# The output stage's tile transposes: from TensorE to VectorE's 32x32 blocks, with the rest of the turn done by the store to DRAM

## The chip, the core and the metric

The kernel runs on one core of a Trainium2 chip. The core has five engines with queues of their own: TensorE (PE, matrix products; PEld is its weight load), VectorE (DVE), ScalarE (ACT), GpSimd (POOL) and SyncE (SP, which here issues DMAs only), and 16 DMA engines that all queues share. The metric is device time in microseconds. The time before is 2435.05 us, the median of three runs (2434.82 to 2436.79).

## The reference, cut to what matters

One layer of a hybrid streaming encoder, for 2048 prompt rows and 8 x 16 sample rows that share the parameters: 17 tiles of 128 rows, 1024 features. A gated DeltaNet group and a short convolution make a 1024-wide row per token. Then, in float32:

```python
mix = jnp.concatenate([o, sc_out.astype(x.dtype)], axis=-1) @ w_o
x = x + rmsnorm(mix, norm_mix_post)

h = rmsnorm(x, norm_ffn_pre)
f = (jax.nn.silu(h @ w_gate) * (h @ w_up)) @ w_down
x = x + rmsnorm(f, norm_ffn_post)
```

The change lies between the second and the last but one of these lines: h, scaled by norm_ffn_pre, has to stand with features on the partitions (transposed) for the products with w_gate and w_up.

## The kernel before

The kernel goes through three parts: projection and recurrence (to about 860 us), the output stage (17 tiles, lines 1116 to 1433), and the feed-forward part (gate and up products in three groups of row tiles, lines 1297 to 1545, then the down products).

**The output stage.** `o_load(t)` (1155) has SP load the mixed rows of tile t into `mr` (one buffer, two halves) and the rows of x into `xo` (two buffers). `o_tile(t)` (1169) casts and splits `mr` into high and low parts (`mix_split`, 1127: ScalarE casts `mh`, VectorE subtracts to `ml`; three buffers each), loads for t+1, and runs 48 products of 128x128 with 128x512 into two PSUM banks, one of `psd` (three banks) and one of `tbank` (two). Then ScalarE sums the squares (1185), VectorE and GpSimd form the factor (`rstd`, 151), and VectorE scales (1190) and adds into `xo` (1191), which ScalarE's queue stores as `x2d` (1192). `o_rows` (1198) makes h of it: squares (1200), factor, `hx = xo * r` (1204). Then come eight TensorE transposes of 128x128 into two PSUM banks (1210), two evictions by VectorE which multiply by the norm weights `g_ffn` on the way (1211) into `ht` (one buffer), and one store from ScalarE's queue into the DRAM tile `hTd` (1214), in runs of 128 floats.

**hTd and its readers.** The 17 tiles form three groups of 6, 6 and 5 (`FGROUPS`); each has one `hTd` with features on the partitions. `ffn_load` (1297) reads it back, eight loads per group, each of 128 features by all rows of the group. The feed-forward products use seven matrix combinations instead of eight (names B11, T3, T1, T2, B21, T4, B22): `ffn_sums` and `ffn_prep` (1308, 1320) form sums and differences of blocks of h and split each into high and low parts.

**The order.** The first group is loaded after tile 6 and is prepared in seven steps, one after each of tiles 7 to 13 (1350 to 1355), each step ordered behind the last tile's work on ScalarE and VectorE by `issue_after`. Groups 1 and 2 are loaded inside the loop over f of the group before (f = 4 to 11), and their sums are formed at f = 12, 14, 16 and 18. The last tile's `o_rows` runs after the first step of the feed-forward loop (1507). In each step f (`gate_up`, 1437) ScalarE copies three partial products out of PSUM (1448 to 1450) before TensorE adds four more products each into those banks (1454 to 1456); two SiLUs follow (1462, 1467), the second marked `gmark["A"]`. Each engine runs its own instructions in order; the order between them is made by a scheduler from the program's order and these marks.

Of the kernel before, what the change touches and what calls it, by code (L numbers as in the profile page):

```python
# [9 lines left out]
F32 = mybir.dt.float32  # L10
F32R = mybir.dt.float32r
BF16 = mybir.dt.bfloat16
AF = mybir.ActivationFunctionType
# [4 lines left out]
P = 128  # L18
D = 1024
KD = D // P  # L20
# [49 lines left out]
FGROUPS = [list(range(0, 6)), list(range(6, 12)), list(range(12, 17))]  # L70
# [27 lines left out]
def kernel(  # L98
# [24 lines left out]
    nc = tc.nc  # L123
    V, A, G, T = nc.vector, nc.scalar, nc.gpsimd, nc.tensor

    const = ctx.enter_context(tc.tile_pool(name="const", bufs=1))
    dram = ctx.enter_context(tc.tile_pool(name="dram", bufs=1, space=DRAM))
# [1 line left out]
    mixo = [dram.tile([P, H, P], F32, name=f"mixo{t}") for t in range(NT)]  # L129
    mixs = [dram.tile([P, 4, len(g) * P], F32, name=f"mixs{gi}") for gi, g in enumerate(GROUPS)]  # L130
    wsplit = [dram.tile([P, 2, KD, P], F32, name=f"wsplit{j}") for j in range(28)]
    hTd = [dram.tile([P, KD, len(g) * P], F32, name=f"hTd{gi}") for gi, g in enumerate(FGROUPS)]
    partd = [[dram.tile([len(g) // 2, P, 7, len(c) // 2, P], F32, name=f"partd{gi}_{ch}") for ch, c in enumerate(FCHUNKS)]
             for gi, g in enumerate(FGROUPS)]
    lastd = [dram.tile([P, 2, len(c) // 2, P], F32, name=f"lastd{ch}") for ch, c in enumerate(FCHUNKS)]
# [5 lines left out]
    ident, ones = cst[:, 0:128], cst[:, 128:256]  # L141
# [3 lines left out]
    g_ffn = vec[:, 8:16]  # L145
# [5 lines left out]
    def rstd(small, ss, n, scale, eps, tag):  # L151
        m = small.tile([P, n], F32, tag=tag[0] + "m", name=tag + "m")
        V.tensor_scalar(out=m, in0=ss, scalar1=scale, scalar2=eps, op0=ALU.mult, op1=ALU.add)
        r = small.tile([P, n], F32, tag=tag + "r", name=tag + "r")
        G.tensor_tensor(out=r, in0=m, in1=neghalf[:, :n], op=ALU.pow)
        return r
# [9 lines left out]
    with ExitStack() as ph:  # L166
# [690 lines left out]
        def new_group(gi, hi, lo, rb):  # L857
            tiles = GROUPS[gi]
            g = dict(gi=gi, tiles=tiles, n=len(tiles), npr=sum(t != SAMPLE for t in tiles), hi=hi, lo=lo, rb=rb,
                     kT=[], qT=[], dt=[], ssk=sm("ssk"), ssq=sm("ssq"),  # L860
                     kt=gp.tile([P, H, MAXT, P], F32, tag="kt", name="kt"),
                     vt=gp.tile([P, H, MAXT, P], F32, tag="vt", name="vt"),
                     sz=gp.tile([P, H, W1], F32, tag="sz", name="sz"))
            return g
# [93 lines left out]
        n = len(tiles)  # L958
        c = n * P
# [31 lines left out]
        for w2 in w2s:  # L991
            j = order.pop(0)[0]
# [74 lines left out]
        for gi, tiles in enumerate(GROUPS):  # L1067
            if gi == 1:
                events.setdefault(30, []).append(caches)
            g = new_group(gi, hi, lo, rb)  # L1070
# [6 lines left out]
            c = len(tiles) * P  # L1077
            for slot, j in enumerate(SEQS[min(gi, 2)]):
# [3 lines left out]
                ps = firsts[slot] if early else psd.tile([P, 512], F32, tag="d", name="dbank")  # L1082
                for s, ks in enumerate((range(0, 3), range(3, 6), range(6, 8))):
                    if not early:
                        matmuls(ps, w, hi, lo, c, ks)
                    if s == 2:
                        later = finish_block(j, ps, g)
                        if later:
                            kind, h = BLOCKS[j]
# [16 lines left out]
        for t in sorted(events):  # L1106
            for f in events[t]:
# [8 lines left out]
        op = ps_o.enter_context(tc.tile_pool(name="op", bufs=1, reuse_waits="tile", side="right"))  # L1116
        oa = ps_a.enter_context(tc.tile_pool(name="oa", bufs=1, reuse_waits="tile", side="right"))
        pft = ps_p.enter_context(tc.tile_pool(name="pft", bufs=3, space=PSUM, reuse_waits="tile"))
        gpost = op.tile([P, D], F32, name="gpost")
        ojunk = op.tile([P, 512], BF16, name="ojunk")  # L1120
        spare = [op.tile([P, D], F32, tag="hx", name="hx"), op.tile([P, KD, P], F32, tag="ht", name="ht"),
                 oa.tile([P, KD, P], F32, tag="mr", name="mr")]
        wo = {k: [oa.tile([P, D], F32R, name=f"{nm}{k}") for nm in ("woh", "wol")] for k in reversed(range(KD))}
        woh, wol = ([wo[k][q] for k in range(KD)] for q in range(2))
# [9 lines left out]
        for k in range(KD):  # L1134
            wh, wl = wo[k]
            if k < len(early_w):
                for q, v in enumerate(early_w[k]):
                    a, b = (h4(w[:, 512 * q:512 * q + 512]) for w in (wh, wl))
# [59 lines left out]
        def o_rows(t, xt, ss):  # L1198
            for n in range(2):
                omark["A"] = A.activation(ojunk, xt[:, n * 512:(n + 1) * 512], AF.Square, accum_out=ss[:, 2 + n:3 + n])  # L1200
            V.tensor_add(ss[:, 2:3], ss[:, 2:3], ss[:, 3:4])
            r = rstd(op, ss[:, 2:3], 1, 1.0 / D, EPS, "oy")
            hx = op.tile([P, D], F32, tag="hx", name="hx") if t else spare[0]
            V.tensor_scalar_mul(hx, xt, r)
            ht = op.tile([P, KD, P], F32, tag="ht", name="ht") if t else spare[1]
            for n in range(2):
                ps = pft.tile([P, 512], F32, tag="t", name="ftbank")
                for q in range(4):
                    k = 4 * n + q
                    T.transpose(ps[:, q * P:(q + 1) * P], hx[:, k * P:(k + 1) * P], ident)  # L1210
                V.tensor_mul(ht[:, 4 * n:4 * n + 4, :], ps.rearrange("p (k c) -> p k c", k=4),
                             g_ffn[:, 4 * n:4 * n + 4].unsqueeze(2).broadcast_to([P, 4, P]))
            gi, i = FPLACE[t]
            nc.scalar.dma_start(out=hTd[gi][:, :, i * P:(i + 1) * P], in_=ht)

        for t in range(O_SPLIT):
            o_tile(t)
# [72 lines left out]
    KH = KD // 2  # L1290
    PARTS = ("B11", "T3", "T1", "T2", "B21", "T4", "B22")
    HW = max(len(g) for g in FGROUPS) * P // 2
    with ExitStack() as ph:
        ks = ctx.enter_context(tc.tile_pool(name="ks", bufs=1, reuse_waits="tile"))
        fp = ph.enter_context(tc.tile_pool(name="fp", bufs=1, reuse_waits="tile"))

        def ffn_load(gi, fs):
            hw = len(FGROUPS[gi]) * P // 2
            for k in range(KD):
                h = fs.tile([P, 2 * HW], F32, tag="h", name="fh", bufs=KD)  # L1300
                nc.sync.dma_start(out=h[:, :2 * hw], in_=hTd[gi][:, k, :])
                yield h

        def blocks(gi, hs, k):
            hw = len(FGROUPS[gi]) * P // 2
# [39 lines left out]
        with tc.tile_pool(name="fs", bufs=1, reuse_waits="tile") as fs:  # L1345
            hload = ffn_load(0, fs)
            hs = [next(hload) for _ in range(KH)]
            o_tile(O_SPLIT)
            hs += hload
            prep = ffn_prep(0, hs, fs=fs)  # L1350
            for i in range(len(PARTS)):
                with tc.issue_after(omark["A"].ins), tc.issue_after(omark["V"].ins):
                    hid = next(prep)
                if i + 1 < len(PARTS):
                    o_tile(O_SPLIT + 1 + i)
# [144 lines left out]
        held, first_parts, gmark, fstores = {}, [], {}, []  # L1500
        for gi in range(len(FGROUPS)):
            if gi:
                *_, hid = ffn_prep(gi, hs, t3)
            for f in range(NF):
                gate_up(gi, f, hid, gu_start(gi, f, hid))
                if (gi, f) == (0, 0):
                    omark["last"]()
                    ps_o.close()
                    fd = side.enter_context(tc.tile_pool(name="fd", bufs=1, reuse_waits="tile", side="right"))
                if f == 3 and gi + 1 < len(FGROUPS):  # L1510
                    hload, hs = ffn_load(gi + 1, fd), []
                if gi + 1 < len(FGROUPS):
                    if 4 <= f < 4 + KD:
                        with tc.issue_after(wl[0].ins):
                            hs.append(next(hload))
                    if f in SUMF:
                        with tc.issue_after(gmark["V"].ins):
                            t3 = ffn_sums(gi + 1, hs, fd, t3 if f > SUMF[0] else None, [SUMF.index(f)])
                elif f == 2:
                    side.close()  # L1520
                    dr = late.enter_context(tc.tile_pool(name="dr", bufs=1, reuse_waits="tile", side="right"))
                    c = len(FCHUNKS[0]) // 2
                    a = dr.tile([P, 2, c * P], F32, tag="ar0", name="ar0")
                    with tc.issue_after(wl[0].ins):
                        nc.sync.dma_start(out=a, in_=partd[0][0][0, :, 0:2].rearrange("p i q c -> p i (q c)"))
                    first_parts = [dr.tile([P, 2, c * P], F32R, name=f"as0{i}") for i in range(3)]
                elif f == 4:
                    with tc.issue_after(gmark["A"].ins), tc.issue_after(gmark["V"].ins):
                        for i, b in enumerate(first_parts[:2]):
                            A.copy(b[:, 0], a[:, i])  # L1530
                            V.tensor_sub(b[:, 1], a[:, i], b[:, 0].bitcast(F32))
                    a = dr.tile([P, 2, c * P], F32, tag="ar0", name="ar0")
                    with tc.issue_after(wl[0].ins):
                        nc.sync.dma_start(out=a[:, 0], in_=partd[0][0][1, :, 0].rearrange("p q c -> p (q c)"))
                    dprep += [down_chunk(ch) for ch in dorder]
# [351 lines left out]
```

## Time and profile before

| what | us |
|---|---|
| median of the runs | 2435.05 |
| the profiled execution | 2436.1 |
| its span in the trace | 2434.3 |
| TensorE busy | 2416.4 |
| VectorE busy | 1602.0 |
| ScalarE busy | 1046.9 |
| GpSimd busy | 558.7 |

The trace's span starts with the first instruction and ends with the last; 1.8 us of the execution lie around it. The profile is read in this way: the busy share of an engine is an average over stages; the chain that ended last is followed back from the last instruction and says whose work the end waited for; a group of instructions has its count, its busy time and the mean length of one, then the idle time just before them and what ended it. A TensorE product's length in the trace is modelled and overlaps the next one, so the pace is read from starts. The granted TensorE clock was 0.999 of full speed.

### The profile page before, as it was taken

To read this page: it belongs to the slowest core of one execution; us is meant where nothing else is said; L and a number is where in the kernel's file an instruction comes from. 1 tells how busy PE (TensorE), PEld (TensorE's weight loads), DVE (VectorE), ACT (ScalarE), POOL (GpSimd) and SP (SyncE) were. 2 spreads that over 40 slices of the span, in tenths; PEclk is the share of its full clock that TensorE was granted. 3 is DMA by queue.
4 is the path that set the end of the run, shared out by engine and by line. 5 is a ranking of instruction groups with operands and counts; after the bars stand their busy time and mean duration, and the time that the engine had idled before them with its cause. 6 is when DMAs were issued, how large, how long until landed. Compare 5 with 4: busy or idle time off the path is not lost.

```text
span 2434.3 us, 39291 instructions
## 1 busy us (share of the span) xinstructions
PE 2416.4 (99%) x14358; PEld 2218.9 (91%) x14358; DVE 1602.0 (66%) x3057; ACT 1046.9 (43%) x2341; POOL 558.7 (23%) x667
## 2 busy tenths in 40 slices
PE   9999999999999999999999999999999999999998
PEld 7888889999989988899999999999999988888877
DVE  7875755756667356788788844456556555667787
ACT  6645545546444333443433422234333345333443
POOL 1211000001110000155655200000000035455663
PEclk9999999999999999999999999999999999999999
DMA  8774555766776657698877888878998844333376
GB/s 292 253 244 168 219 208 187 253 218 232 273 252 247 212 181 227 199 339 296 289 260 257 288 263 267 256 242 271 306 298 282 262 151 128 102 121 126 118 242 197
DMA packets 263753, 561.38 MB, mean 231 GB/s; under 512 B 25220, under 2 KB 144712, under 8 KB 246280
## 3 DMA queue, kind: packets, MB, share of 16 engines
q1 hardware_dynamic: 147456, 487.50, 58.8%
q10 hardware_dynamic: 115880, 70.32, 9.6%
q8 instruction: 113, 1.85, 0.3%
q0 software_dynamic: 224, 1.05, 0.1%
q14 instruction: 80, 0.66, 0.1%
HBM read 400.09 MB, written 158.70 MB: 230 GB/s over the span
## 4 chain that ended last, share of the span: by engine, by line
PE 91%; DVE 3%; issue 2%; ACT 2%; POOL 1%; DMA 1%; POOLq 0%; DVEq 0%; SPq 0%; ACTq 0%
PE fbank L1416 34%; PE dbank L323 25%; PE fbank L1603 17%; PE dbank L1181 4%; PE tbank L1181 4%; PE tbank L381 1%; PE gbank L594 1%; PE gbank L601 1%; PE ftbank L1210 1%; PE obank L773 1%; PE gbank L765 1%; DVE sA L1383 1%; PE gbank L781 1%; PE gbank L787 0%; PE obank L795 0%
## 5 line engine op out<-in xcount | busy, mean ns | idle before, releaser
L1416 PE MATMUL fbank<-xh,fw 128*128 128x384 f32 (+1 forms) x3696 | 897.5, 326 | 1.8 <-ACT m L1448 1.5
L1416 PEld LDWEIGHTS fbank<-xh,fw 128*128 128x128 f32 x3696 | 651.0, 188 | 3.1 <-ACT m L1448 2.5
L323 PE MATMUL dbank<-hi,w 128*128 128x384 f32 (+1 forms) x2224 | 650.5, 363 | 0.7 <-ACT w L988 0.7
L1416 PE MATMUL fbank<-xl,fw 128*128 128x384 f32 (+1 forms) x1848 | 601.9, 326 | 0.0
L323 PEld LDWEIGHTS dbank<-hi,w 128*128 128x128 f32 x2224 | 409.6, 188 | 40.5 <-issue 3.6
L1603 PE MATMUL fbank<-dw,as 128*128 128x512 f32 x1785 | 416.1, 391 | 2.8 <-POOL as L1586 1.0
L1603 PEld LDWEIGHTS fbank<-dw,as 128*128 128x128 f32 x1785 | 334.6, 188 | 77.2 <-POOL as L1586 1.4
L323 PE MATMUL dbank<-lo,w 128*128 128x384 f32 (+1 forms) x1112 | 396.5, 357 | 0.0
L1416 PEld LDWEIGHTS fbank<-xl,fw 128*128 128x128 f32 x1848 | 346.9, 188 | 0.0
L323 PEld LDWEIGHTS dbank<-lo,w 128*128 128x128 f32 x1112 | 209.2, 188 | 15.8 <-DVE lo L238 0.4
L1586 POOL TENSOR_TENSOR as<-ar,as 128x256 fp32r<-128x256 f32 (+1 forms) x202 | 174.6, 873 | 182.9 <-ACT as L1583 177.3
L1583 ACT CAST as<-ar 128x256 fp32r<-128x256 f32 (+1 forms) x287 | 118.9, 427 | 208.8 <-PE fbank L1603 156.3
L1556 DVE TENSOR_TENSOR acc<-acc,fbank 128x512 f32<-128x512 f32 x219 | 147.9, 683 | 86.3 <-PE fbank L1603 69.1
L1266 POOL TENSOR_TENSOR dw<-dr,dw 128x512 fp32r<-128x512 f32 x48 | 67.2, 1409 | 513.8 <-ACT dw L1264 513.4
L1391 ACT CAST fw<-rg 128x512 fp32r<-128x512 f32 x124 | 77.2, 623 | 233.8 <-PE fbank L1416 136.1
L327 DVE SCALAR_TENSOR_TENSOR acc<-R,vec,acc 128x512 f32<-128x512 f32 (+2 forms) x180 | 120.7, 672 | 26.9 <-ACT acc L364 21.1
L1464 DVE TENSOR_TENSOR c<-u,fbank 128x384 f32<-128x384 f32 (+1 forms) x66 | 34.8, 528 | 94.8 <-PE fbank L1416 94.8
L1467 ACT ACTIVATE c<-c 128x384 f32<-128x384 f32 (+1 forms) x66 | 33.4, 506 | 106.0 <-DVE c L1466 106.0
L1460 DVE TENSOR_TENSOR m<-m,m 128x384 f32<-128x384 f32 (+1 forms) x44 | 23.1, 526 | 80.2 <-ACT m L1450 80.1
L1392 POOL TENSOR_TENSOR fw<-rg,fw 128x512 fp32r<-128x512 f32 x44 | 64.2, 1460 | 43.8 <-ACT fw L1391 43.4
L1462 ACT ACTIVATE m<-fbank 128x384 f32<-128x384 f32 (+1 forms) x66 | 31.2, 473 | 88.2 <-PE fbank L1416 70.1
L356 POOL COPY hist<-R 128x3 f32<-128x3 f32 x60 | 18.4, 306 | 217.4 <-ACT R L332 172.0
(403 smaller groups left out, 3566.8 us busy)
## 6 DMA issues: line engine op xcount, KB each, us to landing
w<-wsplit SPq DMA_DIRECT2D x105, 1024.0 KB, 5.1
fw<-fsplit SPq DMA_DIRECT2D x188, 512.0 KB, 4.9
fsplit<-fw SPq DMA_DIRECT2D x94, 512.0 KB, 3.8
partd<-pt ACTq DMA_DIRECT2D x86, 384.0 KB, 6.0
rg<-in_w_gu SPq DMA_DIRECT2D x62, 512.0 KB, 4.3
wsplit<-w SPq DMA_DIRECT2D x28, 1024.0 KB, 4.9
ar<-partd SPq DMA_DIRECT2D x43, 384.0 KB, 3.5
wr<-in_w_in SPq DMA_DIRECT2D x32, 512.0 KB, 6.3
```

What stands on the lines that cost most here:

```text
L323: T.matmul(ps[:, :c], l[:, k, :], r[k][:, :c], start=(k == 0 and r is hi and l is wh), stop=(k == KD - 1 and l is wl))
L327: r = V.scalar_tensor_tensor(acc, raw(d), w[:, d:d + 1], acc, op0=ALU.mult, op1=ALU.add)
L1181: T.matmul(pss[n], m_[:, j, :], w_[k][:, n * 512:(n + 1) * 512], start=(k == 0 and ci == 0), stop=(k == KD - 1 and ci == 2))
L1266: e.tensor_tensor(out=w[1], in0=v, in1=w[0].bitcast(F32), op=ALU.subtract)
L1391: A.copy(w[:, 0], v)
L1392: e.tensor_tensor(out=w[:, 1], in0=v, in1=w[:, 0].bitcast(F32), op=ALU.subtract)
L1416: T.matmul(ps, w_[:, c], b_[k][:, :hw], start=(first and k == 0 and ci == 0), stop=(k == KH - 1 and ci == 2), skip_group_check=not first)
L1464: V.tensor_add(c21, u2, b3)
L1556: mark_d["V"] = V.tensor_tensor(out=dst if out is None else out, in0=dst, in1=ps, op=ALU.add)
L1583: ins = mark_d["A"] = A.copy(a[:, 0, :n], v)
L1586: mark_d["V" if e is V else "G"] = e.tensor_tensor(out=a[:, 1, :n], in0=v, in1=a[:, 0, :n].bitcast(F32), op=ALU.subtract)
L1603: ins = T.matmul(ps, a[:, x_, q * P:(q + 1) * P], w[y_], start=(start and q == 0 and ci == 0), stop=(q == c - 1 and ci == 2), skip_group_c ...
```

## The change

In `o_rows` the eight TensorE transposes and the two evictions are replaced by one VectorE transpose of the whole 128x1024 tile. It turns each 32x32 block by itself: afterwards partition 32b + f holds, at column 32j + c, the value of row 32b + c, feature 32j + f. The store finishes the turn: four DMAs per tile instead of one, one for each band of 32 partitions, each of which puts 1024 runs of 32 floats (128 B) where they belong in `hTd`, which is now a plain matrix of features by rows. `ffn_load` reads the same bytes as before. The norm weights are no longer applied at the eviction: ScalarE multiplies each loaded block of 128 features by its weights (`ffn_gain`), ahead of the first two preparation steps for group 0, and one block per step f = 5 to 12 for groups 1 and 2.

```diff
-    hTd = [dram.tile([P, KD, len(g) * P], F32, name=f"hTd{gi}") for gi, g in enumerate(FGROUPS)]
+    hTd = [dram.tile([D, len(g) * P], F32, name=f"hTd{gi}") for gi, g in enumerate(FGROUPS)]
...
-            ht = op.tile([P, KD, P], F32, tag="ht", name="ht") if t else spare[1]
-            for n in range(2):
-                ps = pft.tile([P, 512], F32, tag="t", name="ftbank")
-                for q in range(4):
-                    k = 4 * n + q
-                    T.transpose(ps[:, q * P:(q + 1) * P], hx[:, k * P:(k + 1) * P], ident)
-                V.tensor_mul(ht[:, 4 * n:4 * n + 4, :], ps.rearrange("p (k c) -> p k c", k=4),
-                             g_ffn[:, 4 * n:4 * n + 4].unsqueeze(2).broadcast_to([P, 4, P]))
+            ht = op.tile([P, D], F32, tag="ht", name="ht") if t else spare[1]
+            V.transpose(ht, hx)
             gi, i = FPLACE[t]
-            nc.scalar.dma_start(out=hTd[gi][:, :, i * P:(i + 1) * P], in_=ht)
+            for b in range(4):
+                c = i * P + 32 * b
+                nc.scalar.dma_start(out=hTd[gi][:, c:c + 32].rearrange("(j f) c -> f j c", f=32),
+                                    in_=ht[32 * b:32 * b + 32].rearrange("f (j c) -> f j c", c=32))
...
-                nc.sync.dma_start(out=h[:, :2 * hw], in_=hTd[gi][:, k, :])
-                yield h
+                nc.sync.dma_start(out=h[:, :2 * hw], in_=hTd[gi][k * P:(k + 1) * P])
+                yield h[:, :2 * hw]
+
+        def ffn_gain(hs, ks):
+            for k in ks:
+                A.activation(hs[k], hs[k], AF.Copy, scale=g_ffn[:, k:k + 1])
...
                 with tc.issue_after(omark["A"].ins), tc.issue_after(omark["V"].ins):
+                    if i < 2:
+                        ffn_gain(hs, range(KH * i, KH * i + KH))
                     hid = next(prep)
...
                 if gi + 1 < len(FGROUPS):
+                    if 5 <= f < 5 + KD:
+                        with tc.issue_after(gmark["A"].ins):
+                            ffn_gain(hs, [f - 5])
                     if 4 <= f < 4 + KD:
```

More of the change, by code (lines that the diff above doesn't have):

```diff
@@ L1120 @@
         ojunk = op.tile([P, 512], BF16, name="ojunk")
-        spare = [op.tile([P, D], F32, tag="hx", name="hx"), op.tile([P, KD, P], F32, tag="ht", name="ht"),
+        spare = [op.tile([P, D], F32, tag="hx", name="hx"), op.tile([P, D], F32, tag="ht", name="ht"),
                  oa.tile([P, KD, P], F32, tag="mr", name="mr")]
```

## The prediction

> **What bounds the kernel now.** I read the page's busy shares and chain of waits first, then a table of stretches around the output stage, then the chain inside it. From the page:
>
> ```profile
> PE 2416.4 (99%) x14358; PEld 2218.9 (91%) x14358; DVE 1602.0 (66%) x3057; ACT 1046.9 (43%) x2341; POOL 558.7 (23%) x667
> ...
> PE 91%; DVE 3%; issue 2%; ACT 2%; POOL 1%; DMA 1%; POOLq 0%; DVEq 0%; SPq 0%; ACTq 0%
> ```
>
> TensorE is busy for 99% of the span, and 91% of the chain that ended last runs through it. So a matmul removed is time removed, for as long as every other engine keeps up. The next table has the first output tiles with all of their stage, the passage into the feed-forward part, tiles 8 to 14 alone, and a piece of the steady feed-forward loop (columns: stretch, its length, then busy us and instructions of PE, PEld, DVE, ACT, POOL, then clock, DMA share, GB/s).
>
> ```profile
> 860.00:1055.00 195.00, 195.00 (x927) 162.75 (x926) 128.41 (x261) 77.45 (x197) 22.21 (x35) 1.00 0.65 208
> 1055.00:1094.00 39.00, 38.55 (x225) 37.94 (x224) 37.62 (x47) 19.42 (x40) 27.57 (x21) 1.00 0.99 371
> ...
> 961.00:1046.20 85.20, 85.20 (x406) 70.99 (x405) 68.77 (x144) 39.55 (x99) 11.41 (x17) 1.00 0.65 213
> ...
> 1160.00:1200.00 40.00, 40.00 (x232) 40.00 (x232) 32.54 (x40) 17.10 (x35) 24.43 (x18) 1.00 0.82 278
> ```
>
> TensorE has no idle time in the stage. VectorE has 81% over tiles 8 to 14 and 96% in the passage, and DMA is full there: the two that could take over. The chain inside the stage (start, us, what) and the transposes' own line:
>
> ```profile
> 936.96 0.87 PE ftbank L1210 x8
> 937.84 0.23 PE dbank L1181
> ...
> 948.54 0.24 PE tbank L1181
> 948.77 0.87 PE ftbank L1210 x8
> 949.64 0.23 PE dbank L1181
> ```
>
> ```profile
> L1210 PE MATMUL ftbank<-cst,hx x136: 271/273/301, 878.2 to 1070.8; 128*128 128x128 f32 x136
> ```
>
> A tile is 948.77 - 936.96 = 11.81 us of TensorE: 0.87 us are its eight transposes, and 10.94 us the 48 products. (The 273 ns are a modelled, pipelined length; the pace is 0.87/8 = 0.109 us.)
>
> **Part 1, the transposes go.** 136 / 8 = 17 tiles x 0.87 = **14.8 us** off TensorE. All of it lies on the chain, the last tile's too, since PE is busy for 38.55 of 39 us where that one runs. The tile's period could fall from 11.81 to 10.94 us.
>
> **Part 2, VectorE.** Out go two PSUM evictions per tile (L1211), in comes one block transpose of 128x1024 from SBUF to SBUF.
>
> ```profile
> L1211 DVE TENSOR_TENSOR ht<-ftbank,vec 128x512 f32<-128x512 f32 x34 | 22.1, 681 | 4.9 <-PE ftbank L1210 4.9
> L1204 DVE TENSOR_SCALAR hx<-xo,oyr 128x1024 f32<-128x1024 f32 x17 | 13.5, 797 | 9.6 <-POOL oyr L155 9.6
> L1148 DVE TENSOR_TENSOR wol<-wor,woh 128x1024 fp32r<-128x1024 f32 x3 | 3.5, 1212 | 0.0
> ```
>
> The trace shows no transpose on VectorE. Instructions of the same 1024 elements take 0.80 us (one operand) and 1.21 us (two); I take 1.21, because one element per step is the plain pace, and keep 0.80 below and 2.42 (two passes) above. VectorE is then 2 x 0.68 - 1.21 = 0.15 us per tile better off. In tiles 8 to 14 it needs 68.77/7 - 0.15 = 9.67 us of 10.94 (88%); at 2.42 it would need 10.9, with nothing left for its waits. The Trainium skill ("VectorE: DVE Perf Modes", section "The three transpose paths") gives 311 ns for a 128x128 bf16 tile on VectorE; eight of them would be 2.49 us, an estimate that pays the fixed part eight times. By it this part would be a loss of 1.13 us per tile. No run here shows it yet.
>
> One wait goes with L1211:
>
> ```profile
> 1054.28 1.29 DVE L1211 TENSOR_TENSOR ht<-ftbank,vec 128x512 f32<-128x512 f32 x2 [4.61 <-PE ftbank L1210]
> ```
>
> Just ahead of the passage, VectorE stands for 4.61 us behind TensorE's transposes of tile 15. The block transpose waits only for hx, so these 4.61 us become slack for the stretch in which VectorE is 96% busy. I book nothing for it; it is what lets the passage move forward as a whole.
>
> **Part 3, ScalarE.** Per tile four store issues replace one, and 24 gain multiplications come in behind the loads of hTd.
>
> ```profile
> L1214 ACTq DMA_DIRECT2D hTd<-ht x17: 520/521/597, 882.0 to 1078.4; - x17
> DMA to landing us min/median/max: 3.5/4.4/10.3
> ```
>
> ```profile
> L237 ACT ACTIVATE hi<-xk,vec x24: 600/616/723, 162.9 to 695.6; 128x384 fp32r<-128x384 f32 x18, 128x512 fp32r<-128x512 f32 x6
> ```
>
> Issues: 3 x 0.52 = 1.6 us more per tile. ScalarE is busy 39.55/7 = 5.7 us per tile in the second half, and less before; with four issues of 0.52 it comes to 7.8 of 10.94. Gains: L237 is the same operation (copy with a scale per partition), about 0.61 us at 384 columns and 0.72 at 512, so an estimated 0.94 at 768 and 0.83 at 640: 16 x 0.94 + 8 x 0.83 = 21.7 us of ScalarE. Eight of them (7.5 us) fall at tiles 7 and 8, ahead of the casts of B11 and T3; products of the next tile hide them, since mh is cast a whole tile ahead. Sixteen lie in the feed-forward loop, one per step f, right behind the SiLU of c12:
>
> ```profile
> 1164.31 0.53 ACT L1467 ACTIVATE c<-c 128x384 f32<-128x384 f32 x1 [5.39 <-DVE c L1466]
> 1164.74 0.46 ACT L1448 COPY m<-fbank 128x384 f32<-128x384 f32 x1
> ...
> 1168.63 0.49 ACT L1462 ACTIVATE m<-fbank 128x384 f32<-128x384 f32 x1 [0.59 <-POOL m L1460]
> ```
>
> ```profile
> PE fbank L1416 <- ACT m L1448: 1.5, 3, 0.7
> ```
>
> Queued behind it is the copy L1448, which TensorE needs before it adds into b1 again: 12 products of 0.173 us (40 us / 232 in the steady loop's row) before about 1168.6, so at 1166.5. The copy ends at 1165.2; a gain of 0.94 leaves 0.4 us. TensorE has waited here three times already. I book **1.0 us** for sixteen gains, with 0 and 8 x 0.94 = 7.5 as ends.
>
> **Part 4, DMA.** The same bytes go out as 4096 packets of 128 B per tile, where there were 1024 of 512 B. Queue rows (packets, MB, share of 16 engines) from five answers, in this order: the first x2d store alone (866 to 880), then the store and the load queue over four tiles (889.7 to 937), then feed-forward stores of 512 B alone (1300 to 1400), then the last group's, with 256 B ones mixed in (1850 to 1950).
>
> ```profile
> q10 hardware_dynamic: 144, 0.52, 11.9%
> ...
> q10 hardware_dynamic: 4736, 4.19, 33.0%
> q1 hardware_dynamic: 2827, 3.87, 25.2%
> ...
> q10 hardware_dynamic: 10608, 5.31, 18.3%
> ...
> q10 hardware_dynamic: 9664, 4.20, 15.5%
> ```
>
> Per engine and tile: loads 0.252 x 47.3/4 = 3.0 us, x2d 0.119 x 14 = 1.7, so hTd is 0.33 x 47.3/4 - 1.7 = 2.2 us, or 35 ns a packet. In the feed-forward part a 512 B packet takes 0.183 x 1600/10608 = 27.6 ns. Of the last row's 9664 packets, 4.20 MB make 6740 of 512 B and 2920 of 256 B; (248 - 186)/2920 = 21 ns for 256 B. No row has 128 B. Going on by half that step gives 18 ns; scaled by 35/27.6, 23. The ends are 7 (by bytes) and 35. I take 20 ns: 256 packets per engine = 5.1 us, with the other 4.7 us 9.8 of 10.94, 90%. DMA itself binds only above (10.94 - 4.7)/256 = 24 ns.
>
> A rule of the Trainium skill speaks against it: "DMA: Bandwidth & Descriptors", section "Specifications", has writes under 512 B done as read-modify-write. The 256 B row does not show that (21 ns against 27.6). If 128 B behaved so, it is the last rival below.
>
> The stricter limit is the single buffer ht. Transpose t+1 waits until all four stores of t have landed, and behind it on VectorE stand the evictions that free PSUM. The loop: transpose 1.2, fixed part of a landing 4.4 - 2.2 = 2.2, data 5.1, which is 8.5 us if nothing else moves; 13.2 if all 4.7 us of other traffic comes between; 10.9 with half of it. That is the edge of 10.94, so some tiles will stall: **1.0 us** booked.
>
> **Sum.** -14.8 + 1.0 + 1.0 = -12.8 us. The profiled execution took 2436.1 us (span 2434.3 and 1.8 around it): 2423.3. The median of the runs is 1.05 us lower, so **2422.3 us**.
>
> **Rivals.**
> *Half the gain.* The helpers don't follow. In the first half the whole chain of casts, evictions and stores is already slower than TensorE:
>
> ```profile
> 943.12 0.52 ACTq L1214 DMA_DIRECT2D hTd<-ht  x1
> ...
> 949.71 0.62 ACT L1130 CAST mh<-mr 128x512 fp32r<-128x512 f32 x1 [3.98 <-PE ftbank L1210]
> ...
> 955.39 0.52 ACTq L1214 DMA_DIRECT2D hTd<-ht  x1
> ```
>
> ```profile
> 955.87 0.68 DVE L1191 TENSOR_TENSOR xo<-xo,tbank 128x512 f32<-128x512 f32 x1
> ```
>
> Its period is 955.39 - 943.12 = 12.27. Over six tiles it would fall behind by 6 x (12.27 - 10.94) = 8 us, while the eviction that ends at 956.55 has until 949.64 + 10.94 = 960.6, 4 us. So 4 us are lost here, and at most as much in tiles 8 to 14 if the transpose costs 2.42: 2422.3 + 4 to 7, about **2428**. Against it: L1211 (1.28 us) leaves this chain.
> *No change.* A 128 B packet costs what a 512 B one does, 27.6 ns: 256 x 27.6 = 7.1, with 4.7 = 11.8 us per tile, today's period: **2434**.
> *Slower.* The ht loop with nearly all other traffic in it. It decides from 11.81 us on, 70% of the 4.7 us between; at 90% it is 12.7, over the 16 intervals 16 x 0.9 = +14: **2449**, 2457 with all. For it: DMA at 90%, and loads and stores share the engines. Against it: the one store lands in 4.4 us today, with the same traffic about it, and half of those are fixed.
> *Read-modify-write.* Two passages, 2 x 27.6 = 55 ns: 14.1 + 4.7 = 18.8 us per tile, 16 x 7 = +112: **2547**.
>
> **How the numbers follow.** Forecast 0.45, half the gain 0.17, no change 0.12, slower 0.23, read-modify-write 0.03. A measurement of this kernel tells about 0.2% (4.9 us) from no change. Faster 0.62, same 0.12, slower 0.26. The forecast's own range is 2419 (both bookings nil) to 2427. The range is 2418 to 2452: below it lies only a gain at the passage that I haven't booked, above it the end of the loop's case and the last rival.
>
> **What would show it.** Right: no L1210, tiles of 10.9 to 11.1 us, packet time of the store queue near 5 us per tile, VectorE's transpose near 1.2 us. Wrong: VectorE waiting for the landing of hTd before its transpose, and PE for an eviction or for mh; L1448 ending TensorE's waits more than some ten times; DMA at 100% through the stage. In the passage, waits of a queue for a store that it shares no data with, of which there is one now, would grow:
>
> ```profile
> SPq L1394 <- DMA hTd<-ht: 4.0, 1, 4.0
> ```

## The result, and the profile after

The changed kernel takes 2454.88 us (median of 5 runs, 2452.53 to 2455.65), the kernel before 2435.05 beside it. The ratio is 1.0079, with a 95% interval of 1.0068 to 1.0091: **19.8 us slower**, where 12.8 us faster was predicted. The end of the predicted range, 2452, lies 3 us below.

The profiled execution has a span of 2453.4 us, 19.1 more than before. First its busy shares and the chain of waits, on the page:

```profile
PE 2410.3 (98%) x14222; PEld 2212.3 (90%) x14222; DVE 1598.2 (65%) x3040; ACT 1070.9 (44%) x2365; POOL 562.3 (23%) x667
...
PE 56%; DVE 2%; DMA 1%; ACTq 1%; ACT 1%; issue 1%; POOL 1%; SPq 0%; POOLq 0%; DVEq 0%
```

TensorE has 136 instructions less (the transposes) and is no longer busy all the time. ScalarE's queue (ACTq), which had 0% of the chain, is now in it. The table of stretches says where (same columns as before the change):

```profile
860.00:1055.00 195.00, 182.67 (x792) 149.31 (x791) 125.62 (x238) 80.36 (x196) 21.82 (x33) 0.97 0.71 191
1055.00:1094.00 39.00, 28.34 (x144) 27.33 (x143) 23.91 (x35) 14.45 (x34) 16.67 (x13) 0.91 0.93 297
1094.00:1380.00 286.00, 280.62 (x1602) 280.15 (x1601) 234.85 (x285) 126.72 (x242) 169.74 (x119) 0.99 0.81 278
```

In the output stage TensorE stands idle for 12.3 of 195 us, in the passage for 10.7 of 39, and its granted clock is below 1.00 in all three. What it waited for (engine, line, what released it: us in total, times, longest):

```profile
PE dbank L1181 <- ACT mh L1130: 10.8, 3, 10.3
PE fbank L1419 <- ACT m L1453: 10.0, 2, 5.4
PE fbank L1419 <- ACT m L1451: 6.0, 2, 4.3
PE tbank L1181 <- DVE xo L1191: 1.8, 2, 0.9
```

The first three rows are ScalarE, in five long waits; the fourth is VectorE, and short. Next, ScalarE's own timeline around the longest of them (start, us, what; in brackets the idle time before):

```profile
945.60 0.19 ACT L1185 ACTIVATION_READ_ACCUMULATOR ojunk<-tbank 128x1 f32 x1
951.23 6.57 ACTq L1210 DMA_DIRECT2D hTd<-ht  x4
957.90 0.63 ACT L1200 ACTIVATE ojunk<-xo 128x512 bf16<-128x512 f32 x1 [12.11 <-DMA hTd<-ht]
...
960.33 3.40 ACT L1303 ACTIVATE fh<-fh,vec 128x768 f32<-128x768 f32 x4
963.63 0.60 ACT L1130 CAST mh<-mr 128x512 fp32r<-128x512 f32 x1
```

ScalarE computes nothing for 12.11 us. It has arrived at tile 6's store, which is in its queue ahead of the squares of tile 7. The tile is turned at 947.50, the first of the four issues begins at 951.23, and **the four take 6.57 us** (5.0 of issues, 1.5 between them), where 2.1 had been reckoned. Then come the squares, the four gains (3.40 us), and only then the cast mh that TensorE wants. In the passage the store holds ScalarE again, now ahead of the copies m:

```profile
1050.93 0.20 ACT L1185 ACTIVATION_READ_ACCUMULATOR ojunk<-tbank 128x1 f32 x1
1054.67 7.84 ACTq L1210 DMA_DIRECT2D hTd<-ht  x4
1062.61 0.63 ACT L1200 ACTIVATE ojunk<-xo 128x512 bf16<-128x512 f32 x1 [11.49 <-DMA hTd<-ht]
...
1069.44 8.52 ACTq L1210 DMA_DIRECT2D hTd<-ht  x4
1078.00 0.48 ACT L1453 COPY m<-fbank 128x384 f32<-128x384 f32 x1 [9.67 <-DMA hTd<-ht]
```

11.49 us are 3.5 of standing at the store until VectorE has turned the tile, and 7.84 of issuing. All 68 issues in one row, with the transpose below it (nanoseconds: min/median/max; first and last start), from the view of the tile ht:

```profile
L1210 ACTq DMA_DIRECT2D hTd<-ht x68: 309/658/4125, 876.9 to 1098.3; - x68
L1206 DVE STREAM_TRANSPOSE ht<-hx x17: 1230/1239/1246, 875.6 to 1094.9; 128x1024 f32<-128x1024 f32 x17
...
DMA to landing us min/median/max: 2.3/4.7/9.7
```

Added up one by one, the 68 issues hold ScalarE's queue for 69.8 us, 4.1 per tile; the 17 of before took 9.0. Within a set the first takes 0.31 us and the second mostly 0.58, up to 1.7, but the third and fourth 0.6 to 4.1. VectorE's waits show how this feeds back:

```profile
DVE oss L1201 <- ACT ojunk L1200: 28.9, 13, 9.4
...
DVE ht L1206 <- DMA hTd<-ht: 0.4, 1, 0.4
```

VectorE waits for the held squares, so it turns the next tile late, and ScalarE stands at that tile's store until then: a loop between two engines whose queues are in order. The buffer ht holds nothing up (0.4 us).

**The sum of the difference.** Over 860 to 1400 us, the gaps between starts of TensorE (those over 0.5 us apart, less a product's own pace) add up to 29.9 us, against 2.6 before. So -14.8 + 27.3 = +12.5 us, of 19.1 measured. The clock after the four longest gaps costs more, in another table of stretches:

```profile
964.30:969.00 4.70, 4.70 (x12) 3.69 (x13) 3.63 (x9) 3.38 (x9) 0.55 (x1) 0.53 0.93 172
...
1068.00:1073.00 5.00, 5.00 (x20) 5.00 (x21) 4.24 (x9) 0.33 (x1) 1.95 (x2) 0.68 0.90 272
...
1078.50:1084.00 5.50, 5.47 (x24) 5.47 (x25) 3.29 (x3) 5.50 (x13) 5.44 (x5) 0.74 0.85 298
...
1102.50:1108.00 5.50, 5.49 (x17) 5.49 (x18) 3.23 (x3) 1.53 (x3) 3.69 (x3) 0.50 0.58 157
```

TensorE is busy there, at a clock of 0.53, 0.68, 0.74 and 0.50: 4.70 x 0.47 + 5 x 0.32 + 5.5 x 0.26 + 5.5 x 0.50 = 8.0 us of its pace lost in these four. That makes +20.5 us, 1.4 more than measured. In the traces, the time from the 1500th feed-forward product (at about 1338 us) to the end is 2.1 us shorter than before, which these terms leave out.

### The profile page after: what moved, and what is told of

The parts are those of the page before. It is cut to its first block, busy times and chain, and to the rows that moved or that the text cites. A ratio compares the mean times of both kernels' runs of the same rounds, so it can differ in the third digit from the quotient of the medians.

```text
span 2453.4 us, 39082 instructions
## 1 busy us (share of the span) xinstructions
PE 2410.3 (98%) x14222; PEld 2212.3 (90%) x14222; DVE 1598.2 (65%) x3040; ACT 1070.9 (44%) x2365; POOL 562.3 (23%) x667
## 4 chain that ended last, share of the span: by engine, by line
PE 56%; DVE 2%; DMA 1%; ACTq 1%; ACT 1%; issue 1%; POOL 1%; SPq 0%; POOLq 0%; DVEq 0%
PE fbank L1419 36%; PE fbank L1609 17%; PE dbank L1181 2%; PE tbank L1181 1%; ACTq L1210 1%; DMA hTd<-ht 1%; DMA fh<-hTd 0%; POOL dw L1263 0%; DVE ht L1206 0%; POOL as L1592 0%; DVE fw L1395 0%; ACT fw L1394 0%; DVE sD L1388 0%; ACT fh L1303 0%; ACT as L1589 0%
## 5 line engine op out<-in xcount | busy, mean ns | idle before, releaser
L1419 PEld LDWEIGHTS fbank<-xh,fw 128*128 128x128 f32 x3696 | 654.9, 189 | 17.5 <-ACT m L1453 10.7
L1463 DVE TENSOR_TENSOR m<-m,m 128x384 f32<-128x384 f32 (+1 forms) x44 | 23.1, 526 | 83.2 <-ACT m L1453 83.0
L1453 ACT COPY m<-fbank 128x384 f32<-128x384 f32 (+1 forms) x66 | 30.6, 463 | 91.4 <-PE fbank L1419 74.0
```

Of the source, the lines that this page charges most:

```text
L1419: T.matmul(ps, w_[:, c], b_[k][:, :hw], start=(first and k == 0 and ci == 0), stop=(k == KH - 1 and ci == 2), skip_group_check=not first)
```

## The experiments

A table of all of them first. "Gaps" are the gaps of TensorE's starts from 860 to 1400 us, and "issues" the time that the issues of hTd's stores took, both added up in the profiled execution, whose span stands before them. Ratios are to runs of the kernel before on the same chip. Three kernels don't compute the same: with runs of 512 B, h is not turned beyond its 32x32 blocks, and without the gains it isn't multiplied by the norm weights; they are here for their time alone.

| kernel | median us | ratio, 95% interval | span | gaps | issues: count, us |
|---|---|---|---|---|---|
| before | 2435.05 | | 2434.3 | 2.6 | 17, 9.0 |
| the change | 2454.88 | 1.0079 (1.0068 to 1.0091) | 2453.4 | 29.9 | 68, 69.8 |
| stores from SP | 2434.56 | 0.9996 (0.9986 to 1.0006) | 2430.6 | 9.2 | 68, 67.5 |
| runs of 512 B (h not turned) | 2429.44 | 0.9975 (0.9966 to 0.9984) | 2427.2 | 7.2 | 68, 39.8 |
| no gains (h not weighted) | 2445.53 | 1.0043 (1.0027 to 1.0060) | 2446.9 | 23.1 | 68, 64.8 |
| gains alone | 2435.24 | 1.0000 (0.9991 to 1.0010) | 2434.6 | 2.9 | 17, 6.4 |
| SP and ScalarE in turn | 2436.88 | 1.0007 (0.9998 to 1.0016) | 2433.8 | 13.8 | 68, 39.6 |
| in turn, gain by row | 2467.61 | 1.0131 (1.0118 to 1.0144) | 2465.3 | 34.8 | 68, 39.5 |
| SP, two buffers ht | 2436.86 | 1.0006 (0.9997 to 1.0014) | 2437.2 | 12.4 | 68, 70.9 |
| 512 B and no gains (neither) | 2427.78 | 0.9969 (0.9957 to 0.9981) | 2422.8 | 6.2 | 68, 35.1 |
| turned at the load | 2430.01 | 0.9979 (0.9970 to 0.9989) | 2426.2 | 8.0 | 35, 24.6 |
| the same, gains on POOL | 2434.53 | 0.9996 (0.9987 to 1.0005) | 2432.7 | 10.8 | 35, 22.7 |
| eight stores of half size | 2473.70 | 1.0160 (1.0143 to 1.0177) | 2471.4 | 44.7 | 136, 87.2 |

The theory after the first look ("theory I") was that ScalarE's queue is held while it hands over the stores' many small packets. Its rivals were the packets' price on the DMA engines, the gains, and ht's single buffer.

**Stores from SP's queue.** Same packets, another issuer.

```diff
-                nc.scalar.dma_start(out=hTd[gi][:, c:c + 32].rearrange("(j f) c -> f j c", f=32),
+                nc.sync.dma_start(out=hTd[gi][:, c:c + 32].rearrange("(j f) c -> f j c", f=32),
...
```

> The changed kernel with the four stores of hTd issued from SP's queue instead of ScalarE's; all else as changed. Theory I (the third and fourth store of a tile hold their issuing queue until the descriptors of the first two have drained, so ScalarE stands 2.5 to 8.5 us per tile and everything behind it is late): ScalarE is free again, TensorE's waits for mh, L1451 and L1453 (26.8 us) mostly go, about 2425 us (2420 to 2432); the long issues move to SP's rows. Theory P (the 128 B packets load the DMA engines): no change, about 2455, with loads late instead. Theory G (the gain multiplications on ScalarE): no change, at least 2450.

It took 2434.56 us, 20 less than the change. So neither the packets on the DMA engines nor their landing made these 20 us: the issuer did. But it isn't the 2425 of theory I. The hold has moved to SP (its timeline, then the row of the issues in the view of hTd):

```profile
942.75 7.25 SPq L1210 DMA_DIRECT2D hTd<-ht  x4
950.10 1.38 SPq L1164 DMA_DIRECT2D xo<-in_x  x1
```

```profile
L1210 SPq DMA_DIRECT2D hTd<-ht x68: 303/592/4067, 876.5 to 1083.5; - x68
```

The load of the next x stands behind those 7.25 us. And here the forecast's loop does bite: VectorE waits for the stores before it turns the next tile.

```profile
DVE ht L1206 <- DMA hTd<-ht: 6.6, 2, 3.6
```

**Runs of 512 bytes.** The same bytes in four stores, in a quarter of the packets.

```diff
-                c = i * P + 32 * b
-                nc.scalar.dma_start(out=hTd[gi][:, c:c + 32].rearrange("(j f) c -> f j c", f=32),
-                                    in_=ht[32 * b:32 * b + 32].rearrange("f (j c) -> f j c", c=32))
+                nc.scalar.dma_start(out=hTd[gi][:, i * P:(i + 1) * P].rearrange("(j f) c -> f j c", f=P)[32 * b:32 * b + 32],
+                                    in_=ht[32 * b:32 * b + 32].rearrange("f (j c) -> f j c", c=P))
```

> The changed kernel with the four stores per tile cut into runs of 512 B instead of 128 B: 32 partitions x 8 runs, 256 packets each instead of 1024, same bytes, same four issues from ScalarE. The rows land untransposed beyond their 32x32 blocks, so h is not turned as the reference needs it. Theory I and theory P: about 2424 us (2420 to 2430), issues 0.3 to 0.6 us each. If the count of issues and not of packets holds the queue: 2445 to 2455. Theory G: at least 2450.

2429.44 us, 25 below the change, and below the kernel before. The issues fall to 39.8 us, with the longest at 2.05 (view of hTd):

```profile
L1209 ACTq DMA_DIRECT2D hTd<-ht x68: 309/475/2051, 876.5 to 1071.7; - x68
```

With issuer, number of stores, bytes and gains unchanged, cutting the stores into four times as many packets, each a quarter as long, costs 25 us. How full the DMA engines are may play a part: the change's longest sets, 7.7 and 8.4 us of issues, lie in the passage, where DMA has a share of 0.93, and there one set of the 512-byte runs took 5.9 us too (at 1067.5, against 1.2 to 3.0 elsewhere). No run separates the two.

**No gains, and gains alone.** The first leaves out `ffn_gain`. The second keeps TensorE's transposes and the single store of before, copies out of PSUM without weights, and adds the 24 gains. The edit of the first:

```diff
-                    if i < 2:
-                        ffn_gain(hs, range(KH * i, KH * i + KH))
...
-                    if 5 <= f < 5 + KD:
-                        with tc.issue_after(gmark["A"].ins):
-                            ffn_gain(hs, [f - 5])
```

> The changed kernel without the 24 gain multiplications (h isn't scaled by norm_ffn_pre). Theory G: the whole loss goes, about 2424 us. Theory I: only the 3.4 us that they stood ahead of the cast of mh in TensorE's 10.3 us wait, and a little in the feed-forward loop: 2446 to 2453.

> One part alone: TensorE's transposes, PSUM evictions (now plain copies) and the single store in 512 B runs as before, but the norm weights multiplied at the load as in the change. Theory G: 2450 or more. Theory I: 2435 to 2439, the gains cost 0 to 4 us.

Alone the gains cost nothing (1.0000). In the change they cost 9.4 us (2454.88 - 2445.53). TensorE's longest wait without them, from the view of its waits, beside 10.3 us with them:

```profile
PE fbank L1417 <- ACT m L1449: 10.9, 4, 5.8
PE dbank L1181 <- ACT mh L1130: 7.4, 2, 7.2
```

The 3.1 us between are about the four gains (3.40 us) ahead of mh. ScalarE hides them as long as it isn't late already. Another 4.7 us lie at the copies m in the passage (16.0 us of waits with the gains, 11.3 without), where no gain runs; why is not shown. What is left, 10 us slower than before, is the held queue.

**SP and ScalarE in turn.** Two stores of a tile from each.

```diff
-                nc.scalar.dma_start(out=hTd[gi][:, c:c + 32].rearrange("(j f) c -> f j c", f=32),
+                (nc.scalar if b % 2 else nc.sync).dma_start(out=hTd[gi][:, c:c + 32].rearrange("(j f) c -> f j c", f=32),
...
```

> The four 128-byte-run stores of a tile go out alternately: bands 0 and 2 from SP's queue, 1 and 3 from ScalarE's; the 24 gains stay on ScalarE. Theory Q (each queue takes about two such stores, 2048 descriptors, before it holds the issuer: in the run of the change the first two issues of a set took 0.31 and 0.58 us, the third up to 4.1): both queues issue their two in about 0.9 us a tile, no issue above 1.5 us, ScalarE is never held, the waits of PE on ScalarE's mh and m fall from 26 us to under 5, and the time is 2420 to 2430. Rival R (the hold is the rate at which the 16 shared DMA engines drain such runs, whoever issues): issues of 2 to 4 us stay on both queues, PE still waits some 10 us for ScalarE, and the time is 2436 to 2448. Rival H (ht's only buffer, seen with all stores on SP, where VectorE waited 6.6 us for the stores, decides): 2430 to 2436, the same as with all stores on SP.

The issues fall to 39.6 us, and their medians to 0.56 and 0.36 (view of hTd):

```profile
L1210 SPq DMA_DIRECT2D hTd<-ht x34: 303/556/3232, 877.0 to 1074.1; - x34
L1210 ACTq DMA_DIRECT2D hTd<-ht x34: 309/362/1862, 877.0 to 1075.3; - x34
```

So most of the hold belongs to a queue, as theory Q has it: two queues with two stores each are held far less than one with four. The time doesn't follow: 2436.88 is in the range of rival R. Single issues of 1.9 and 3.2 us remain, and TensorE still waits for ScalarE:

```profile
PE fbank L1419 <- ACT m L1451: 8.0, 4, 5.8
PE dbank L1181 <- ACT mh L1130: 5.1, 2, 4.8
```

The sum of the issue times alone therefore doesn't give the time: with almost the same sum, the runs of 512 B took 7 us less. That it matters where a store stands in the two queues, and what is behind it, is a reading that no run isolates.

**In turn, with the gain on the row tile.** A second attempt at the gains, with two edits at once: VectorE multiplies by the weights' row while it makes hx (ScalarE's 24 gains go, and the row is loaded once), and the squares' thrown-away output goes into hx to make room for that row.

```diff
...
-            V.tensor_scalar_mul(hx, xt, r)
+            V.scalar_tensor_tensor(hx, xt, r, gfr, op0=ALU.mult, op1=ALU.mult)
...
-                omark["A"] = A.activation(ojunk, xt[:, n * 512:(n + 1) * 512], AF.Square, accum_out=ss[:, 2 + n:3 + n])
+                omark["A"] = A.activation(hx[:, :512], xt[:, n * 512:(n + 1) * 512], AF.Square, accum_out=ss[:, 2 + n:3 + n])
...
```

> As the split of the stores over SP and ScalarE, and the gain moves back into the row tile: VectorE multiplies by r and by the gain's row in one scalar-tensor-tensor of 128x1024 (the trace of the change has 0.75 us for 128x512, so about 1.5 against 0.81 us, 0.7 us more on VectorE per tile of 10.9) and ScalarE's 24 multiplies go; the squares' thrown-away output is written into hx. Theory Q with gains harmless when the queue is free (gains alone cost nothing beside the transposes of before): same time as the split within 2 us, 2418 to 2430. Rival G (the four gains of 3.4 us that stand ahead of mh are what is left): 3 to 6 us below the split. Rival V (VectorE's chain from the squares to the store grows by 0.7 us and delays what is queued behind it): 3 us or more above the split.

2467.61 us, 31 above the split, far more than the 0.48 us that the longer VectorE instruction costs per tile (1.285 against 0.81). Its waits from 880 to 1055 us show late loads (ScalarE's, then those of SP's queue):

```profile
ACT mh L1130 <- DMA mr<-mixo: 37.2, 10, 4.9
```

```profile
SPq L1165 <- DMA x2d<-xo: 72.9, 11, 8.8
```

SP stands at the load of x (36.6 us in the split, 72.9 here), and mr is behind it. Which of the two edits put it there is open.

**Two buffers for ht, stores from SP.** As with stores from SP, and the squares' output goes into hx here too, to make room for the second buffer.

```diff
...
-            ht = op.tile([P, D], F32, tag="ht", name="ht") if t else spare[1]
+            ht = op.tile([P, D], F32, tag="ht", name="ht", bufs=2) if t else spare[1]
...
```

> All four stores from SP, as before in this study (2434.6, VectorE waited 6.6 us for ht's only buffer, PE 9.2 us in all between 860 and 1400 us), now with two buffers for ht (the squares' thrown-away output goes into hx to make the room). Theory H (ht's only buffer is what kept the version with all stores on SP from its gain): no wait of VectorE for the stores, PE's waits fall by 4 us or more, 2426 to 2431. Rival S (SP, held up to 7 us by a set, brings its loads of mr and h late, which is where PE's waits come from): ht's wait goes and the time stays within 2 us of 2434.6.

VectorE's wait for the stores is gone, and the time is 2436.86, no better than with one buffer (2434.56). Rival S is nearer. ht's buffer was a wait, but not the one that set the time, as far as the second edit costs nothing by itself. This kernel has one of the two edits of the slow version above and isn't slow; its stores come from another queue, though, so that doesn't settle which of them cost the 31 us.

**Runs of 512 bytes and no gains.** Both edits shown above, together.

> Both suspects out at once: the four stores of a tile write runs of 512 bytes (256 packets each instead of 1024; the rows beyond the 32x32 blocks are not turned), and no gain is multiplied (h is not scaled by norm_ffn_pre). What is left of the change is TensorE without its transposes, and VectorE's one transpose. Theory F (the 14.8 us of TensorE's time are there to be had, and only the held issues and the gains took them back): PE's waits of over 0.5 us between 860 and 1400 us sum to under 4 us (2.6 before, 7.2 with the long runs alone), and the time is 2419 to 2425. Rival L (something else of the shorter period binds: loads of mr, VectorE's chain, the DMA engines at 1055 to 1094 us): no better than the long runs alone, 2427 to 2431, with waits of 7 us again.

The lowest median of all, 2427.78, but in rival L's range (2427 to 2431) and not in theory F's, and the gaps sum to 6.2 us, where F had under 4. Against the runs of 512 B alone it is 1.7 us, inside the intervals: with the queue mostly free, the gains cost nothing that can be told. The profiled execution took 2424.59, the least of six. Its waits:

```profile
PE fbank L1416 <- ACT m L1449: 4.2, 1, 4.2
PE fbank L1416 <- DVE xo L1191: 1.5, 1, 1.5
```

Its account: -14.8 for the transposes, 6.2 - 2.6 = +3.6 for gaps, and 3.5 x 0.49 = +1.7 for the clock of 0.51 from 1071.5 to 1075, behind the longer wait, make -9.5. The span differs by 2422.8 - 2434.3 = -11.5, the median by -7.6. So most of the 14.8 us is there to be had; two waits in the passage, and the clock behind one, take a part back.

**Turned at the load.** Tiles 0 to 5 store as in the change. From tile 6 on, ht goes out as it lies, in one store of 128 rows of 4 KB. The runs of 128 bytes are placed by the loads of groups 1 and 2 instead, from SP, while the feed-forward part runs.

```diff
...
+            if gi:
+                nc.scalar.dma_start(out=hTd[gi][i * P:(i + 1) * P], in_=ht)
-            for b in range(4):
+            for b in range(0 if gi else 4):
...
+                    turned = hTd[gi].rearrange("(g f) d -> f g d", f=32)
+                    for j in range(4):
+                        c = k * P + 32 * j
+                        nc.sync.dma_start(out=h[32 * j:32 * j + 32, :2 * hw].rearrange("f (g c) -> f g c", c=32),
+                                          in_=turned[:, :, c:c + 32])
...
```

> Tiles 0 to 5 (the first FFN group) store as the change does; tiles 6 to 16 store ht as it lies, one store of 128 rows of 4 KB, and the 32-token runs are put in place at the loads of FFN groups 1 and 2, four loads of 32 partitions for each of 8 tiles, from SP's queue, while gate-up runs. By theory I (packets of a store that ScalarE issues hold its queue) the sets of 2.5 to 8.5 us from tile 6 on become one issue under 1 us, PE's stalls after the first one go (29.9 us in the change, of which 10.3 at 953 us has the four gains in it and may stay in part), and the time is 2424 to 2434, if SP has room for 64 issues in the FFN stage. Rival S (SP is held by the same packets there and its weight loads come late): new waits of PE for DMA or fw after 1094 us, and 2440 or more.

**2430.01 us, 0.9979 (0.9970 to 0.9989)**: the same computation, faster than both kernels. The rows of the view of hTd, then the first two of the stretches shown for the change:

```profile
L1304 SPq DMA_DIRECT2D fh<-hTd x64: 384/506/2755, 1091.9 to 1537.1; - x64
L1212 ACTq DMA_DIRECT2D hTd<-ht x24: 309/580/2442, 876.6 to 937.7; - x24
L1209 ACTq DMA_DIRECT2D hTd<-ht x11: 326/326/345, 950.8 to 1068.8; - x11
```

```profile
860.00:1055.00 195.00, 190.57 (x840) 157.51 (x839) 133.79 (x252) 87.74 (x213) 32.15 (x40) 0.99 0.70 216
1055.00:1094.00 39.00, 38.40 (x222) 38.08 (x221) 38.72 (x44) 16.68 (x34) 24.65 (x18) 1.00 0.89 342
```

The eleven stores from tile 6 on cost ScalarE 0.33 us each. TensorE is busy for 38.40 of 39 us in the passage, where the change had 28.34. SP had room for the 64 loads: the feed-forward part shows one new wait of 2.3 us.

**The first group's gains on POOL**, in that version (`ffn_gain` takes the engine):

```diff
...
-                        ffn_gain(hs, range(KH * i, KH * i + KH))
+                        ffn_gain(hs, range(KH * i, KH * i + KH), G)
```

> As the version that turns at the load, and the eight gains of the first FFN group run on POOL (by its 1.2 to 1.6 us for tensor-tensors of 128x384 and 128x512 some 1 to 2 us each) instead of ScalarE. Theory G (the four gains of 3.4 us ahead of mh are what is left of the stall near 953 us): 3 us or more below the version with gains on ScalarE. Rival K (POOL's queue also holds the tile's two rstd steps, on which VectorE and so PE's banks wait): 2 us or more above it.

4.5 us slower. A gain takes POOL 2.2 us, more than the 1 to 2 expected, as the groups by line show:

```profile
L1313 POOL TENSOR_SCALAR fh<-fh,vec 128x768 f32<-128x768 f32 x8 | 17.7, 2233 | 5.1 <-DMA fh<-hTd 5.1
```

That agrees with rival K's sign and size, but its mechanism, the rstd steps queued behind, wasn't isolated.

**Eight stores of half size.** Twice the issues, the same packets.

```diff
-                nc.scalar.dma_start(out=hTd[gi][:, c:c + 32].rearrange("(j f) c -> f j c", f=32),
-                                    in_=ht[32 * b:32 * b + 32].rearrange("f (j c) -> f j c", c=32))
+                for m in range(2):
+                    d = slice(512 * m, 512 * m + 512)
+                    nc.scalar.dma_start(out=hTd[gi][d, c:c + 32].rearrange("(j f) c -> f j c", f=32),
+                                        in_=ht[32 * b:32 * b + 32, d].rearrange("f (j c) -> f j c", c=32))
```

> As the change, but each of the four stores of a tile is cut in two: eight issues of 512 packets of 128 bytes instead of four of 1024, the same bytes and packets, all on ScalarE's queue. Theory I (the hold follows the packets handed over, not the issues): a tile's issues still sum to some 2.5 to 8.5 us, since the four more come at about 0.3 us each only where nothing is held; single issues get shorter (under 4 us, mean about 0.4 instead of 0.66), and the time is 2453 to 2462. Rival C (each issue costs on its own, by its count or by the wait for one of the semaphores that the stores share): a tile's issues sum to twice as much, 5 to 15 us, and the time is 2470 or more.

2473.70 us: theory I alone, which allowed 2462, falls, and the time is rival C's. Its sums are not: the issues went from 69.8 to 87.2 us, far from double.

```profile
L1212 ACTq DMA_DIRECT2D hTd<-ht x136: 309/518/4255, 876.0 to 1137.6; - x136
```

An issue that is not held takes 0.31 us as the first of a set and about 0.50 after it, so 8 cost 3.8 us per tile, where 4 of the full size cost 0.31 + 3 x 0.58 = 2.05. The change's 69.8 us are thus 35 for the issues by their count and 35 of hold; here they are 65 and 22. In three sets the queue also stood idle between issues, for 5.0, 8.5 and 3.3 us. What the store waited for there, the trace doesn't name; the semaphores that the stores share are a possible cause, not tested. These 16.8 us are nearly all of the 18.8 by which this kernel is slower than the change, so its time doesn't show by itself what more stores cost. The lengths of the issues do: **two things hold ScalarE, the number of stores, by 0.3 to 0.6 us each, and the packets, which hold the later issues of a set.**

## Why the prediction was wrong, by its own steps

- **Part 1, the transposes: right.** L1210's matmuls are gone, and the kernel with 512-byte runs and no gains has a span that lies within 2 us of the 14.8 less its gaps and the clock behind them.
- **Part 2, VectorE: right.** The block transpose takes 1.24 us where 1.21 was taken; neither the 0.80 nor the 2.42 held. The 2.49 estimated from the 311 ns of the Trainium skill ("VectorE: DVE Perf Modes", "The three transpose paths") is twice what the trace has. That the wait of 4.61 us would become slack for the passage was wrong in effect: from 860 to 1110 us VectorE waits 28.9 us for held squares, against 5.4 before.
- **Part 3, ScalarE's issues: this is the step that failed.** It said "Issues: 3 x 0.52 = 1.6 us more per tile", with "four issues of 0.52". It took the duration of one store of 1024 packets, issued alone, as a price per issue. Measured are 4.1 us per tile instead of 2.1, and up to 8.4 us in a set in the passage. The average is not the worst of it: 7.8 of 10.94 us busy still leaves room, but a set of 6.6 to 8.5 us stands in one piece, in order, ahead of the squares and mh. The step counted the issues as load on an engine and didn't ask what is queued behind them.
- **Part 3, the gains: right in price, wrong in cover.** One takes 0.92 us at 768 columns and 0.82 at 640, against an estimated 0.94 and 0.83 (four in a row overlap, 3.40 us), and alone they cost nothing. Of the eight at tiles 7 and 8 it said that "products of the next tile hide them, since mh is cast a whole tile ahead". With ScalarE 12 us late, that cover was gone, and the gains cost 9.4 us. The 1.0 us booked for those in the feed-forward loop didn't show: behind 1110 us TensorE has no wait for a copy m in the change.
- **Part 4, the packets: too dear.** From 889.7 to 937 us, the queue rows of the change are these (packets, MB, share of 16 engines):

```profile
q10 hardware_dynamic: 17872, 4.30, 42.3%
q1 hardware_dynamic: 3352, 4.23, 30.9%
```

  Less four stores of x2d, (0.423 x 47.3 - 4 x 1.67) x 16 / (17872 - 4 x 144) = 12.3 ns per packet of 128 B, where 20 was taken (7 to 35). It is an estimate, since the price of x2d is the one of before. The kernel with runs of 512 B has, in the same stretch and worked out in the same way, (0.335 x 47.3 - 4 x 1.67) x 16 / (5961 - 4 x 144) = 27.2 ns per packet:

```profile
q10 hardware_dynamic: 5961, 4.69, 33.5%
```

  The read-modify-write rival (55 ns) is out, and so is the no-change one (27.6). DMA is not full in the output stage (0.71); in the passage it has 0.93, where before had 0.99.
- **The loop over ht: wrong in the change.** VectorE waited 0.4 us for it, where 1.0 was booked and 14 us made up the slower rival. That rival gave 2449 to 2457, the right time for a wrong reason: two buffers didn't help even where the wait was real, with the stores on SP.
- **What would show it.** Of its signs of failure, "PE for [...] mh" came. The sign set for L1448, more than ten waits, did not: the copies L1451 (L1448 before) and L1453 ended four waits, but of up to 5.4 us. Both point to ScalarE, whose queue, held by its own issues, was a mechanism of no rival.

A rule of the Trainium skill ("DMA: Bandwidth & Descriptors", section "Issuing engines are not separate DMA queues") says that issuing a DMA takes a time that is usually small beside the DMA itself. Here it isn't: sets of four took 2.5 to 8.5 us, with a median landing of 4.7.

Open are the 3.7 us between the end of tile 6's transpose (947.50) and its first issue, the idle stretches between issues (1.5 us there, 3.3 at tile 6 with runs of 512 B, more with half-size stores), and the slow version with the gain by row. So of the 12.11 us at tile 6, 5.2 have no cause shown; the sets in the passage are issues nearly throughout (7.7 of 7.84 us, 8.4 of 8.52).

## What to carry to other kernels

In these runs a store cut into many short runs was paid by the engine that issues it: price it from its packets and from its place in that engine's in-order queue, and ask what stands behind it. If runs must be short, let them be issued where nothing urgent follows; here that was the load, on SP, in a stage with slack. An added cost that is hidden today (the gains) is hidden only while its engine is on time.

## What the runs showed of the hardware

- **Issues are held though their data are ready.** An issue of 1024 packets of 128 B from ScalarE took 0.31 us as the first of a set (0.36 at most) and up to 4.1 us as the third. The hold moves with the issuer (67.5 us on SP) and shrinks when two queues share the stores (39.6) or the packets are a quarter (39.8).
- **A 128 B packet cost an estimated 12.3 ns of a DMA engine**, against 21 for 256 B and 27.2 to 27.6 for 512 B. So a short packet is cheaper than a long one, but the same bytes cost 1.8 times as much in runs of 128 B (4 x 12.3 = 49 ns against 27.2).
- **After a stall of 4.3 to 10.3 us, TensorE's granted clock was 0.50 to 0.74 over the next 5 us.** The Trainium skill ("TensorE: Matmul & The Clock Gate", "What's actually happening") has the clock at half after an idle window of some 3.4 us; the trace agrees (0.50 from 1102.5 to 1108, after 5.4 us idle).
